# Where the two halves of an attention head's values are added: DVE out of the bank, or POOL in SBUF

## The chip, the cores and the metric

The kernel runs on one core of a Trainium2 chip. The metric is the device time of one execution in microseconds (us), the median of several runs. Five engines work side by side, each through its own instructions in order: TensorE (PE, with its weight loads shown as PEld), VectorE (DVE), ScalarE (ACT), GpSimd (POOL) and SyncE (SP, which issues DMAs here). They wait for each other through semaphores. Matrix products land in the banks of PSUM; all else lies in SBUF.

## The reference, cut to what matters

The program computes two layers of an encoder over 512 tokens of width 1024. In each layer, 12 token heads and 4 memory heads of width 64 attend, their outputs are concatenated, and one more product (`w_o`) follows. Layer 0 attends in a band of +-128 tokens with a sink logit, layer 1 globally with rotary and a norm on queries and keys.

```python
s = jnp.einsum('bqhgd,bkhd->bhgqk', qblk, k, preferred_element_type=jnp.float32) * ATTN_SCALE
p = jax.nn.softmax(s, axis=-1)
return jnp.einsum('bhgqk,bkhd->bqhgd', p.astype(v.dtype), v)
...
o = jnp.concatenate([tok, mo], axis=-1) @ w_o[i]
x = x + rms_norm(o, g_mix_post[i])
h = rms_norm(x, g_ffn_pre[i])
gu = h @ w_gate_up[i]
f = (jax.nn.silu(gu[..., :D_FF]) * gu[..., D_FF:]) @ w_down[i]
x = x + rms_norm(f, g_ffn_post[i])
```

## The kernel before, in words

Every operand of a product is split into a high part and a low part (`split`, L274: an ACT copy `hi` at L280 and a DVE subtraction `lo` at L284; for some weights both are on POOL, L278 and L282), and a product is three matmuls (L270 to L272). The order of the work in the attention stage is a list sorted by a position in heads, from the numbers in `PACE`; PE runs its instructions in the order in which that list is written, while the other engines' instructions are ordered by a scheduler.

One head passes through these steps, numbered 0 to 15 in each layer (12 to 15 are the memory heads, which have half as many keys and are paced closer together):

- `score` (L535) or `score_mem` (L566): PE writes the scores (L548, L549; L578, L579), DVE takes the minimum (L554, L559 or L580), ACT the exponential with the row sum (L560, L583).
- `normalise` (L589): DVE's reciprocal `rd` (L596), then four POOL multiplications of the probabilities `p` (L599). The four are the four blocks of 128 queries.
- `turn` (L602): PE transposes `p` (L609) into a bank `tp`, and `tp` is split into `th` on ACT (L280) and `tl` on DVE (L284). `turn` comes once for each block of 128 keys.
- `value` (L616): PE accumulates values times `th` and `tl` (L623, L624) in the bank `o`, of which there is one (tag `pv`, `bufs=1`). The values are stored as [high | low] in 64 + 64 columns, so that partitions 0 to 63 of `o` hold the high half of the output and 64 to 127 the low half. They must be added: ACT copies one half to the other's partitions in SBUF (`tmp`, L631, two buffers), and DVE adds it to the half that it reads from the bank, into `tok` (L632). Only then is the bank free for the next head's first L623.

Two heads share a slice `tok[:, k]` (k = 0 to 7). In `heads_out` (L765), once both are there, `part(k)` splits that slice into the operand of the `w_o` product, also called `th` in the profile: an ACT copy `th<-tok` (L280) and a DVE subtraction `th<-tok,th` (L284). The products of k = 0 to 5 with three of the four token blocks are mixed into the attention stage; `mix_out` (L796) does the fourth block of k = 0 to 5, then all four of k = 6, then of k = 7.

So ACT's queue holds, mixed: the exponentials, the splits of `tp`, the copies L631 and the splits of `tok`. DVE's holds the minima, the low parts and L632. POOL's holds L599 and, early in layer 0, splits of weights.

Of the kernel before, what the change touches and what calls it, by code (L numbers as in the profile page):

```python
# [13 lines left out]
OP = mybir.AluOpType  # L14
# [165 lines left out]
class Trunk:  # L180
# [435 lines left out]
    def value(self, hd, j):  # L616
        nc = self.nc
        if j == 0:
            hd["o"] = self.ps.tile([P, S], F32, tag="pv", name="o", bufs=1)
        o, hg = hd["o"], hd["hg"]  # L620
        c0, c1, th, tl = hd[j]
        last = j == hd["nk"] - 1
        nc.tensor.matmul(o[:, c0:c1], hd["v"](j), th, start=(j == 0), stop=False, skip_group_check=True)  # L623
        nc.tensor.matmul(o[:, c0:c1], hd["v"](j), tl, start=False, stop=last, skip_group_check=True)  # L624
        if not last:
            return
        odd = hg % 2
        here = slice(HD, P) if odd else slice(0, HD)
        there = slice(0, HD) if odd else slice(HD, P)
        tmp = self.core.tile([P, S], F32, tag="tmp", name="tmp", bufs=2)  # L630
        nc.scalar.activation(tmp[here], o[there], AF.Copy)  # L631
        nc.vector.tensor_add(self.tok[here, hg // 2], o[here], tmp[here])  # L632

    def axial(self, buf):

# [610 lines left out]
```

## Time and profile before

| | us |
|---|---|
| median of 3 runs (lowest to highest) | 1124.85 (1124.82 to 1125.47) |
| the profiled execution | 1125.38 |
| span of its instructions | 1123.6 |
| PE busy in the span | 1096.6 (98%) |
| DVE busy | 844.3 (75%) |
| ACT busy | 660.8 (59%) |
| POOL busy | 203.8 (18%) |

Times in rows of the trace are microseconds from the start of the span. In a row of the timeline stand the start, the time from the first start to the last end of a run of equal instructions, the engine, the line, what is written and read, the shape and the count; in square brackets the idle time of that engine ahead of it and what ended it. In a row of the groups stand the count, then the summed busy time and the mean duration of one in ns, then idle time. In the view of one tile, the lists below the rows give us in total and the number of times. The attention stages run from about 60 to 176 us (layer 0) and from about 600 to 745 us (layer 1).

### The profile page before, as it was taken

How to read it: one execution, taken by the hardware profiler on the slowest of the kernel's cores; microseconds unless marked ns; L12 is line 12 of the kernel's file. 1: busy time of each engine (PE TensorE's matmuls, PEld its weight loads, DVE VectorE, ACT ScalarE, POOL GpSimd, SP SyncE). 2: the span in 40 equal slices, each digit the busy share in tenths (PEclk: the TensorE clock that was granted, in tenths of full speed). 3: DMA queues.
4: the chain of work that ended last, by engine and by line, in shares of the span. 5: the costliest groups of instructions: out<-in, count | busy, mean ns of one | idle time of the engine just before them, and what ended most of it. 6: DMA issues, size and time to landing. Idle time of an engine off the chain costs nothing.

```text
span 1123.6 us, 19533 instructions
## 1 busy us (share of the span) xinstructions
PE 1096.6 (98%) x7463; PEld 1003.6 (89%) x7463; DVE 844.3 (75%) x1431; ACT 660.8 (59%) x1343; POOL 203.8 (18%) x348
## 2 busy tenths in 40 slices
PE   8999999999999999999999999999999999999997
PEld 7889988899889989998898888878999899899985
DVE  5688885899557867885788998758996478669854
ACT  6678984666445634663467878756665255345631
POOL 5693331102000000000343543312000000000001
PEclk9999999999999999999999999999999999999999
DMA  6521015443753382325543221145136223423243
GB/s 237 194 81 47 20 57 206 169 132 114 243 180 112 112 283 76 112 79 195 179 150 113 76 76 39 38 150 188 39 113 217 65 76 114 149 62 103 85 166 112
DMA packets 38685, 139.29 MB, mean 124 GB/s; under 512 B 4416, under 2 KB 4800, under 8 KB 38464
## 3 DMA queue, kind: packets, MB, share of 16 engines
q1 hardware_dynamic: 38448, 137.91, 36.4%
q8 instruction: 58, 0.95, 0.3%
q14 instruction: 35, 0.29, 0.1%
q10 hardware_dynamic: 144, 0.14, 0.0%
HBM read 119.16 MB, written 18.87 MB: 123 GB/s over the span
## 4 chain that ended last, share of the span: by engine, by line
PE 68%; DVE 6%; ACT 3%; POOL 2%; issue 2%; DVEq 0%; POOLq 0%; ACTq 0%
PE ps L978 12%; PE ps L979 12%; PE ps L980 12%; PE ps L271 9%; PE ps L270 9%; PE ps L272 9%; PE tp L609 1%; PE o L624 1%; PE o L623 1%; PE s L548 1%; DVE nm L559 1%; PE s L549 1%; DVE wlo L284 1%; POOL r L299 1%; ACT whi L280 1%
## 5 line engine op out<-in xcount | busy, mean ns | idle before, releaser
L280 ACT ACTIVATE whi<-raw 128x1024 fp32r<-128x1024 f32 (+2 forms) x186 | 157.9, 863 | 185.2 <-PE ps L980 81.8
L284 DVE TENSOR_TENSOR wlo<-raw,whi 128x1024 fp32r<-128x1024 f32 (+2 forms) x178 | 175.9, 998 | 74.8 <-ACT whi L280 71.7
L978 PE MATMUL ps<-sf,whi 128*128 128x256 f32 x640 | 179.9, 281 | 0.2
L979 PE MATMUL ps<-sf,wlo 128*128 128x256 f32 x640 | 179.7, 281 | 0.0
L980 PE MATMUL ps<-sf,whi 128*128 128x256 f32 x640 | 179.7, 281 | 0.0
L270 PE MATMUL ps<-whi,f 128*128 128x512 f32 x352 | 137.2, 390 | 0.0
L271 PE MATMUL ps<-wlo,f 128*128 128x512 f32 x352 | 137.1, 390 | 0.0
L272 PE MATMUL ps<-whi,f 128*128 128x512 f32 x352 | 137.0, 389 | 0.0
L980 PE MATMUL ps<-a,whi 128*128 128x256 f32 x480 | 134.4, 280 | 0.0
L978 PE MATMUL ps<-a,whi 128*128 128x256 f32 x480 | 134.3, 280 | 0.0
L979 PE MATMUL ps<-a,wlo 128*128 128x256 f32 x480 | 133.8, 279 | 0.0
L978 PEld LDWEIGHTS ps<-sf,whi 128*128 128x128 f32 x640 | 121.1, 189 | 1.1 <-ACT p L984 0.6
L979 PEld LDWEIGHTS ps<-sf,wlo 128*128 128x128 f32 x640 | 121.4, 190 | 0.5
L980 PEld LDWEIGHTS ps<-sf,whi 128*128 128x128 f32 x640 | 121.4, 190 | 0.0
L308 POOL TENSOR_SCALAR e<-sso 128x1 f32<-128x1 f32 x8 | 3.4, 424 | 566.1 <-ACT junk L303 565.9
L270 PE MATMUL ps<-whi,hT 128*128 128x256 f32 (+1 forms) x320 | 98.8, 309 | 0.9 <-ACT whi L292 0.9
L271 PE MATMUL ps<-wlo,hT 128*128 128x256 f32 (+1 forms) x320 | 93.9, 294 | 2.6 <-DVE wlo L284 1.9
L599 POOL TENSOR_SCALAR p<-p,rd 128x256 f32<-128x256 f32 (+2 forms) x128 | 78.2, 630 | 99.8 <-DVE rd L596 50.3
L272 PE MATMUL ps<-whi,hT 128*128 128x256 f32 (+1 forms) x320 | 93.7, 293 | 0.0
L979 PEld LDWEIGHTS ps<-a,wlo 128*128 128x128 f32 x480 | 90.5, 188 | 0.2
L978 PEld LDWEIGHTS ps<-a,whi 128*128 128x128 f32 x480 | 90.4, 188 | 0.2
L980 PEld LDWEIGHTS ps<-a,whi 128*128 128x128 f32 x480 | 90.1, 188 | 0.0
(201 smaller groups left out, 2735.0 us busy)
## 6 DMA issues: line engine op xcount, KB each, us to landing
raw<-in_wgu_dram SPq DMA_DIRECT2D x48, 512.0 KB, 4.4
raw<-in_wd_dram SPq DMA_DIRECT2D x44, 512.0 KB, 4.4
rb<-in_wgu_dram SPq DMA_DIRECT2D x40, 512.0 KB, 3.6
raw<-in_wo_dram SPq DMA_DIRECT2D x17, 512.0 KB, 3.6
raw<-in_wq_dram SPq DMA_DIRECT2D x16, 512.0 KB, 5.0
xt<-x SPq DMA_DIRECT2D x12, 512.0 KB, 4.5
raw<-in_wm_dram SPq DMA_DIRECT2D x8, 512.0 KB, 4.3
x<-y SPq DMA_DIRECT2D x8, 512.0 KB, 3.0
```

Of the source, the lines that this page charges most:

```text
L270: mm(out, lh, rh, start=first, stop=False)
L271: mm(out, lh, rl, start=False, stop=False)
L272: mm(out, ll, rh, start=False, stop=last)
L280: nc.scalar.activation(hi, src, AF.Copy)
L284: nc.vector.tensor_sub(lo, src, hi.bitcast(F32))
L299: g.tensor_tensor(r, r, self.mhalf[:, :r.shape[1]], op=OP.pow)
L548: nc.tensor.matmul(s[:, :n], qi, hd["ka"]()[:, k0 * P:k1 * P], start=True, stop=False)
L549: nc.tensor.matmul(s[:, :n], qi, hd["kb"]()[:, k0 * P:k1 * P], start=False, stop=True)
L599: self.pooled = nc.gpsimd.tensor_scalar(hd["p"][z][:, :n], hd["p"][z][:, :n], rd[:, z:z + 1], 1.0, op0=OP.mult, op1=OP.mult)
L978: mm(out, wh[:, s], rh, start=start and k == 0, stop=False, skip_group_check=True)
L979: mm(out, wl[:, s], rh, start=False, stop=False, skip_group_check=True)
L980: mm(out, wh[:, s], rl, start=False, stop=k == 3, skip_group_check=True)
```

## The change

The addition of the two halves leaves DVE. DVE copies its half from the bank to `tok` (L632), and POOL then adds `tmp` to it in SBUF, in place (a new line, L633; lines behind it move by one). The ACT copy L631 stays. That is 32 DVE additions replaced by 32 DVE copies of the same shape, and 32 POOL additions of 64x512 more.

```diff
         nc.scalar.activation(tmp[here], o[there], AF.Copy)
-        nc.vector.tensor_add(self.tok[here, hg // 2], o[here], tmp[here])
+        nc.vector.tensor_copy(self.tok[here, hg // 2], o[here])
+        nc.gpsimd.tensor_tensor(self.tok[here, hg // 2], self.tok[here, hg // 2], tmp[here], op=OP.add)
```

PE's instructions keep their order, and so do those of DVE and ACT but for one swap in each layer. POOL's change. Three places follow; in square brackets stand the engines whose counts an instruction waits for.

DVE in layer 0, from the L632 of head 11 on, before:

```order
L632 TENSOR_TENSOR tok<-o,tmp 64x512 [waits Activation_49]
L284 TENSOR_TENSOR tl<-tp,th 128x512 [waits DVE_49,Activation_49]
L580 TENSOR_REDUCE nm<-s 128x2 [waits PE_49]
L284 TENSOR_TENSOR th<-tok,th 128x512 [waits Activation_49]
L284 TENSOR_TENSOR tl<-tp,th 128x512 [waits Activation_49]
```

and after:

```order
L632 COPY tok<-o 64x512 [waits Activation_49]
L284 TENSOR_TENSOR tl<-tp,th 128x512 [waits DVE_49,Activation_49]
L580 TENSOR_REDUCE nm<-s 128x2 [waits PE_49]
L284 TENSOR_TENSOR th<-tok,th 128x512 [waits Activation_49]
L284 TENSOR_TENSOR tl<-tp,th 128x512 [waits DVE_49,Activation_49]
```

The copy stands where the addition stood. It reads nothing that ACT writes, and it still waits for ACT: the program makes it wait for the same count as before, the one that L631 of that head raises, and not for PE.

POOL in layer 0, at memory heads 14 and 15, before:

```order
L599 TENSOR_SCALAR p<-p,rd 128x256 [waits DVE_49]
L599 TENSOR_SCALAR p<-p,rd 128x256 [waits PE_49,Activation_49] x3
L599 TENSOR_SCALAR p<-p,rd 128x256 [waits DVE_49,PE_49]
L599 TENSOR_SCALAR p<-p,rd 128x256 [waits PE_49,Activation_49]
L599 TENSOR_SCALAR p<-p,rd 128x256 [waits Activation_49]
L599 TENSOR_SCALAR p<-p,rd 128x256 [waits PE_49,Activation_49]
```

and after, with the additions of heads 11, 12, 13 and of 14 and 15:

```order
L633 TENSOR_TENSOR tok<-tok,tmp 64x512 [waits DVE_49,Pool_49]
L599 TENSOR_SCALAR p<-p,rd 128x256 [waits DVE_49,PE_49,Pool_49]
L599 TENSOR_SCALAR p<-p,rd 128x256 [waits PE_49]
L599 TENSOR_SCALAR p<-p,rd 128x256 [waits PE_49,Activation_49] x2
L633 TENSOR_TENSOR tok<-tok,tmp 64x512 [waits DVE_49]
L599 TENSOR_SCALAR p<-p,rd 128x256 [waits DVE_49,PE_49]
L599 TENSOR_SCALAR p<-p,rd 128x256 [waits PE_49,Activation_49]
L599 TENSOR_SCALAR p<-p,rd 128x256 [waits Activation_49]
L599 TENSOR_SCALAR p<-p,rd 128x256 [waits PE_49,Activation_49]
L633 TENSOR_TENSOR tok<-tok,tmp 64x512 [waits DVE_49,Pool_49]
L633 TENSOR_TENSOR tok<-tok,tmp 64x512 [waits DVE_49] x2
```

The addition of head 13 stands behind the four multiplications of head 15, and each addition waits for DVE's copy.

ACT at the end of layer 0's attention, with the split of slice k = 7 (`th<-tok`) behind the last L631, before:

```order
L280 ACTIVATE th<-tp 128x512 [waits PE_49,Activation_49]
L631 ACTIVATE tmp<-o 64x512 [waits PE_49,Activation_49]
L280 ACTIVATE th<-tok 128x512 [waits DVE_49]
L280 ACTIVATE whi<-raw 128x512 [waits DMAHW7_49,PE_49]
L280 ACTIVATE whi<-raw 128x512
```

and after:

```order
L280 ACTIVATE th<-tp 128x512 [waits PE_49,Activation_49]
L631 ACTIVATE tmp<-o 64x512 [waits PE_49,Activation_49]
L280 ACTIVATE whi<-raw 128x512 [waits DMAHW7_49,PE_49]
L280 ACTIVATE th<-tok 128x512 [waits Pool_49]
L280 ACTIVATE whi<-raw 128x512
```

The split of `tok` now waits for POOL, and one piece of a weight's split has moved ahead of it; the same swap stands on DVE and in layer 1. The other splits of `tok` on ACT (k = 4, 5, 6) also wait for POOL where they waited for DVE, at the same places of ACT's queue as before.

## The prediction

> **What bounds the kernel now.** I read the page's head first:
>
> ```profile
> span 1123.6 us, 19533 instructions
> ...
> PE 1096.6 (98%) x7463; PEld 1003.6 (89%) x7463; DVE 844.3 (75%) x1431; ACT 660.8 (59%) x1343; POOL 203.8 (18%) x348
> ```
>
> PE is busy for 1096.6 of 1123.6 us, so 27 us of idle time is all that a change of order can win, and a microsecond that PE newly waits is a microsecond of the result. The change touches no PE instruction; it acts through what PE waits for. Then the view of the tile `tmp`, with the two instructions that empty the bank and those who wait for them:
>
> ```profile
> L631 ACT ACTIVATE tmp<-o x32: 589/594/597, 80.3 to 739.1; 64x512 f32<-64x512 f32 x32
> L632 DVE TENSOR_TENSOR tok<-o,tmp x32: 670/689/696, 81.0 to 739.7; 64x512 f32<-64x512 f32 x32
> ...
>   PEld o L623: 3.4, 6
>   PE o L623: 2.3, 5
> ```
>
> The bank is emptied in two steps of 0.59 and 0.69 us, one behind the other, and in all 32 heads PE's matmuls wait 2.3 us for that; the 3.4 us are waits of weight loads, which PE may or may not feel. So the bank's release is worth between 2.3 and 5.7 us at the very most.
>
> How full the engines are in the two attention stages shows the sum of a view by windows (80 to 176 and 615 to 745 us):
>
> ```profile
> sum 226.00, PE 219.20 PEld 192.19 DVE 190.41 ACT 185.89 POOL 87.11; mean PE 109.60 PEld 96.10 DVE 95.21 ACT 92.94 POOL 43.55
> ```
>
> PE idles 6.8 us of 226, DVE is busy for 84%, ACT for 82%, POOL for 39%. ACT and DVE work close behind PE, so a delay in their queues can reach it.
>
> **The DVE step.** The prices of the new operations come from the groups by shape:
>
> ```profile
> L282 POOL TENSOR_TENSOR wlo<-raw,whi 128x512 fp32r<-128x512 f32 x16 | 21.3, 1353 | 2.2 <-ACT whi L280 2.1
> ...
> L599 POOL TENSOR_SCALAR p<-p,rd 128x512 f32<-128x512 f32 x48 | 35.6, 759 | 29.6 <-DVE rd L596 24.3 <-PE s L579 5.4
> ```
>
> ```profile
> L415 DVE CAST kmb<-tp 128x512 fp32r<-128x512 f32 x4 | 2.7, 677 | 0.3 <-PE tp L414 0.3
> ```
>
> The nearest row to the new copy is that cast out of a bank: 512 columns in 0.68 us, hardly below the addition's 0.69. Twice the pace would show there as 0.34, and it does not. I take 0.68: 32 x 0.01 us, and only where PE waits; 0.1 us gained.
>
> What would matter is the start of the copy. "Side by side" means that it starts with L631 instead of behind it. The built program says no: the copy waits for the same count of ACT as the addition did. So the bank comes free when it did, the 2.3 us stay, and the change amounts to one more step behind an unchanged chain. [...]
>
> **The POOL step.** No row shows a POOL addition of 64x512. By columns its nearest row is L282, two inputs of 512 columns in SBUF: 1.35 us. From below it is bounded by L599, one input of 512 columns, 0.76 us. Half the partitions need not mean half the time: L631, at 64 partitions, takes 0.59 us, and ACT's copies of 128x512 below take 0.60 to 0.63. I take 1.35.
>
> That is 32 x 1.35 = 43 us more on POOL, in 226 us where it works 87. First, what is queued behind it on POOL: the next head's multiplications. In layer 0, head 2's copy and head 4's multiplications, with PE's first reads of these:
>
> ```profile
> 95.77 0.68 DVE L632 TENSOR_TENSOR tok<-o,tmp 64x512 f32<-64x512 f32 x1
> ...
> 97.31 2.11 POOL L599 TENSOR_SCALAR p<-p,rd 128x256 f32<-128x256 f32 x4 [4.47 <-ACT th L280]
> ...
> 100.77 0.39 PE L609 MATMUL tp<-cst,p 128*128 128x128 f32 x2
> ```
>
> The addition can start at 96.5 and ends at 97.85, so the multiplications start 0.5 us later. PE's reads at 100.77 need the first two of four, done by about 98.4: 2.3 us to spare. Token heads repeat this; cost 0, up to an addition of about 2.8 us.
>
> Second, who waits for POOL: the splits of `tok` on ACT. For k = 0 to 3 they come long after their heads. For k = 5 and 6 (in layer 1 for k = 4 too) they stand right behind the pair's second head, and ACT waits with all that is queued behind it. Place A, layer 0, k = 5:
>
> ```profile
> 158.40 0.69 DVE L632 TENSOR_TENSOR tok<-o,tmp 64x512 f32<-64x512 f32 x1 [1.17 <-ACT tmp L631]
> ...
> 159.13 0.63 ACT L280 ACTIVATE th<-tok 128x512 fp32r<-128x512 f32 x1
> ...
> 160.33 0.68 DVE L284 TENSOR_TENSOR th<-tok,th 128x512 fp32r<-128x512 f32 x1
> ...
> 160.41 0.60 ACT L280 ACTIVATE th<-tp 128x512 fp32r<-128x512 f32 x1 [0.65 <-PE tp L609]
> ...
> 162.51 1.85 POOL L599 TENSOR_SCALAR p<-p,rd 128x256 f32<-128x256 f32 x4 [5.13 <-DVE rd L596]
> ...
> 162.57 0.68 DVE L632 TENSOR_TENSOR tok<-o,tmp 64x512 f32<-64x512 f32 x1 [0.16 <-ACT tmp L631]
> ...
> 163.19 0.69 DVE L284 TENSOR_TENSOR tl<-tp,th 128x512 fp32r<-128x512 f32 x1
> ...
> 164.33 0.39 PE L624 MATMUL o<-tl,vm 128*128 128x512 f32 x1
> ...
> 164.56 0.60 PE L609 MATMUL tp<-cst,p 128*128 128x128 f32 x4
> ```
>
> The addition runs from 159.13 to 160.48, ACT's split starts at 160.51 instead of 159.13 and ends at 161.14. ACT's next is 0.6 us late. DVE's low half of the slice moves from 160.33 to 161.17, 0.84 late; DVE has no gap behind it, so the reciprocal and with it POOL's multiplications at 162.51 are 0.84 late and end at 165.20. The last of PE's four transposes at 164.56 starts at about 164.9 and needs the last of them: 0.3 late. L632 at 162.57 had waited 0.16 for ACT, so it and `tl` at 163.19 are 0.68 late, and L624 waits from 164.33 to 164.56. The two overlap; with the start behind a semaphore A costs 0.4 us.
>
> Place B, k = 6 of layer 0:
>
> ```profile
> 165.98 1.85 POOL L599 TENSOR_SCALAR p<-p,rd 128x256 f32<-128x256 f32 x4 [1.62 <-DVE rd L596]
> ...
> 167.57 0.63 ACT L280 ACTIVATE th<-tok 128x512 fp32r<-128x512 f32 x1
> ...
> 168.24 0.69 DVE L284 TENSOR_TENSOR th<-tok,th 128x512 fp32r<-128x512 f32 x1
> ...
> 169.15 0.60 ACT L280 ACTIVATE th<-tp 128x512 fp32r<-128x512 f32 x1 [0.95 <-PE tp L609]
> ...
> 169.79 0.69 DVE L284 TENSOR_TENSOR tl<-tp,th 128x512 fp32r<-128x512 f32 x1 [0.86 <-ACT th L280]
> ...
> 170.41 0.68 DVE L632 TENSOR_TENSOR tok<-o,tmp 64x512 f32<-64x512 f32 x1
> ...
> 171.15 0.50 PE L623 MATMUL o<-th,vm 128*128 128x512 f32 x1 [0.49 <-DVE tok L632]
> ```
>
> Here POOL is still at head 15's multiplications, which stand ahead of the addition: 167.83 + 1.35 = 169.2. DVE's low half moves from 168.24 to 169.87, `tl` from 169.79 to 170.57, L632 from 170.41 to 171.24: 0.83 late, and PE at 171.15 already waits for just that. What A left on the multiplications (0.65 late, of which PE's own 0.4 comes off) adds 0.25: B costs 1.05 us.
>
> Layer 1, k = 5 (place C), k = 6 (place D) and the end of the stage:
>
> ```profile
> 724.45 0.63 ACT L280 ACTIVATE th<-tok 128x512 fp32r<-128x512 f32 x1
> ...
> 725.84 0.47 ACT L583 ACTIVATE p<-s,nm 128x256 f32<-128x256 f32 x1 [0.75 <-DVE nm L580]
> ...
> 732.35 1.85 POOL L599 TENSOR_SCALAR p<-p,rd 128x256 f32<-128x256 f32 x4 [3.34 <-DVE rd L596]
> ...
> 733.66 0.64 ACT L280 ACTIVATE th<-tok 128x512 fp32r<-128x512 f32 x1
> ...
> 734.17 0.50 PE L624 MATMUL o<-tl,vm 128*128 128x512 f32 x1 [0.16 <-DVE tl L284]
> ...
> 736.55 0.68 DVE L632 TENSOR_TENSOR tok<-o,tmp 64x512 f32<-64x512 f32 x1 [1.25 <-ACT tmp L631]
> ...
> 737.38 0.47 PE L623 MATMUL o<-th,vm 128*128 128x512 f32 x1 [0.68 <-DVE tok L632]
> ```
>
> ```profile
> 741.14 0.69 DVE L284 TENSOR_TENSOR th<-tok,th 128x512 fp32r<-128x512 f32 x1 [0.70 <-ACT th L280]
> ...
> 745.86 0.40 PE L270 MATMUL ps<-whi,th 128*128 128x512 f32 x1
> ```
>
> C: the split goes from 724.45 to 725.85, the exponential behind it from 725.84 to 726.4, 0.55 late; between there and 734.17, where PE waits for DVE anyway, some of it is taken up by idle time. Between 0 and 0.55 I take 0.35. D: multiplications until 734.20, addition until 735.55, split until 736.2, DVE's low half (0.68 us) until 736.95, L632 0.37 late, and PE at 737.38 waits for it: 0.37. The last slice, k = 7, costs nothing: its low half would end some 1.4 us after 741.83, and the first matmul of k = 7 is the one at 745.86 (30 matmuls behind the last L624). Layer 1, k = 4 falls among token heads, whose 2.3 us to spare cover 1.4: 0.
>
> **DVE beside POOL.** Two low-half subtractions of 256 columns, the first with both inputs in SBUF, the second with one in a bank:
>
> ```profile
> L284 DVE TENSOR_TENSOR q<-qx,q 128x256 fp32r<-128x256 f32 x32 | 16.9, 528 | 4.0 <-ACT q L280 3.6
> ...
> L284 DVE TENSOR_TENSOR tl<-tp,th 128x256 fp32r<-128x256 f32 x24 | 10.0, 417 | 1.9 <-ACT th L280 1.7
> ```
>
> The first are 0.11 us slower, 3.5 us in 32. If that is POOL working beside them, 43 us more on 87 make half as much again: 1.8 us, and about as much for the rotary steps, 3.5 us of DVE time. DVE idles 16% of the stages, so most is covered: between 0 and 3.5 us I take 0.4. [...]
>
> **The sum.** 0.4 + 1.05 + 0.35 + 0.37 + 0.4 - 0.1 = 2.5 us. The profiled execution took 1125.38 us (its span and 1.8 us around it), which gives 1127.9; it lies 0.5 us above the median, so against 1124.85 the forecast is **1127.3 us**, with A to D uncertain by half: 1126.2 to 1128.6.
>
> **Rivals.**
>
> - *The two reads do overlap.* The bank would be free 0.6 us earlier and the splits would be 0.7 us late instead of 1.4: 2.3 us gained or a little more, about 1122.3. The program's wait speaks against it. 0.06.
> - *The addition is short* (not slower). ACT idles 0.65 us ahead of 160.41 and 0.95 ahead of 169.15. If POOL takes less than about 0.75 us for 64 partitions, the splits end before ACT's next instruction is due, and A to D vanish: 1124.9 to 1125.3. L599's 0.76 is near that point; that it has one input speaks against. 0.24.
> - *POOL becomes the bound.* If addition and DVE stretch each other, to 2 us each and 3.5 us of DVE, A to D grow by 0.65 each and 1 us of DVE time shows: 1127.3 + 2.6 + 0.6, about 1130.3. L282's mean was taken in just such company, which speaks against much more. 0.12.
>
> **How the numbers follow.** The forecast case has the remaining 0.58. About 0.2%, 2.25 us, is what a measurement of this kernel can tell from no change, so slower begins at 1127.1. Of the forecast's own range some two thirds lie above: slower 0.58 x 0.64 + 0.12 = 0.49, same 0.58 x 0.36 + 0.24 = 0.45, faster 0.06. The range from 1124.9 to 1130.0 takes in the short addition and most of the stretched one.
>
> **What would show it.** In the profile after: L632 as a copy of 0.67 to 0.69 us that starts behind L631 (if it starts with it, the first rival); L633 at 1.2 to 1.5 us on 64x512 (at 0.75 or less, the second); ACT's `th<-tok` waiting for POOL about seven times, over 1 us each; PE's idle time in the two stages up by about 2 us, at the memory heads and not at the token heads; q<-qx,q above 528 ns. PE waiting for L599 at token heads would make the place wrong, and a stage after the attention that takes up the delay would make the sum wrong.

## The result and the profile after

The changed kernel takes 1132.41 us (median of 4 runs, 1132.28 to 1132.91) against 1124.84 us before (4 runs beside it): ratio 1.0067, 95% interval 1.0049 to 1.0084, so 7.6 us slower. The forecast was 1127.3 us with a range up to 1130.0: the direction was right, the size was not. One execution of a later kernel (e6_dose1) had a mean granted clock of 0.56 and took 1795 us; it is left out of that kernel's time below, and all others ran at 0.996 or more.

The head of the page after:

```profile
span 1130.7 us, 19550 instructions
...
PE 1098.1 (97%) x7463; PEld 1003.5 (89%) x7463; DVE 852.1 (75%) x1431; ACT 660.7 (58%) x1343; POOL 244.3 (22%) x380
```

POOL has 40.5 us more work, as forecast (43). But DVE has 7.8 us more, although its copies were to be no longer than its additions. The view of the tile `tok`, after:

```profile
L632 DVE COPY tok<-o x32: 669/689/696, 80.6 to 747.0; 64x512 f32<-64x512 f32 x32
L633 POOL TENSOR_TENSOR tok<-tok,tmp x32: 1274/1287/1322, 82.2 to 747.8; 64x512 f32<-64x512 f32 x32
...
  POOL tok L633: 9.6, 7
...
  PE o L623: 3.4, 5
```

The copy takes 0.689 us, just what the addition took; POOL's addition takes 1.29; seven splits of `tok` on ACT wait for POOL, 1.4 us each; PE's wait for the bank grew from 2.3 to 3.4 us. None of that is 7.6 us. To find the place I compared the start of the same matmul in both traces (PE's order did not change):

| the matmul | before | after | later by |
|---|---|---|---|
| L270, near the start | 8.00 | 7.70 | -0.30 |
| L624, token heads, layer 0 | 85.52 | 86.97 | 1.45 |
| L609 | 98.08 | 101.39 | 3.31 |
| L609 | 111.81 | 116.33 | 4.52 |
| L609 | 119.01 | 124.63 | 5.62 |
| L609, memory heads (place A) | 164.88 | 170.92 | 6.04 |
| L623 (place B) | 171.15 | 178.08 | 6.93 |
| L623, token heads, layer 1 | 666.80 | 673.44 | 6.64 |
| L623, memory heads (place C) | 733.54 | 740.46 | 6.92 |
| L623 (place D) | 737.38 | 744.66 | 7.28 |

So 5.9 us are lost in token heads 0 to 7 of layer 0 (from 0.30 us early to 5.62 late), where the forecast had almost nothing, and 2.0 us at the four places that it named. What DVE does in that stretch shows the groups by shape, before (78 to 125 us):

```profile
L423 DVE TENSOR_TENSOR rt<-qx,cst 128x32 f32<-128x32 f32 x5 | 2.1, 415 | 0.0
L425 DVE TENSOR_TENSOR qx<-qx,rt 128x64 f32<-128x64 f32 x5 | 1.8, 362 | 0.1
L595 DVE TENSOR_TENSOR den<-den,es 128x4 f32<-128x4 f32 x7 | 1.4, 199 | 0.2
L424 DVE TENSOR_TENSOR qx<-qx,cst 128x64 f32<-128x64 f32 x5 | 1.3, 270 | 0.0
...
L422 DVE TENSOR_TENSOR rt<-qx,cst 128x32 f32<-128x32 f32 x5 | 1.0, 195 | 0.0
```

and after (78 to 131 us):

```profile
L422 DVE TENSOR_TENSOR rt<-qx,cst 128x32 f32<-128x32 f32 x5 | 5.3, 1058 | 0.0
...
L424 DVE TENSOR_TENSOR qx<-qx,cst 128x64 f32<-128x64 f32 x5 | 2.4, 475 | 0.0
L425 DVE TENSOR_TENSOR qx<-qx,rt 128x64 f32<-128x64 f32 x5 | 2.3, 451 | 0.1
L595 DVE TENSOR_TENSOR den<-den,es 128x4 f32<-128x4 f32 x7 | 2.2, 320 | 0.2
...
L423 DVE TENSOR_TENSOR rt<-qx,cst 128x32 f32<-128x32 f32 x5 | 1.3, 267 | 0.0
```

L422 to L425 are the rotary step of the next four heads' queries (layer 0 has one too, on 16 of a head's 64 columns); in this stretch of layer 0 it comes five times, once in each of heads 0 to 4. They, L595 and the low part `q<-qx,q` read two operands in SBUF. L422 went from 0.20 to 1.06 us. With that low part (0.42 to 0.50 us, seven of them) the six groups, each count times the change of its mean, have 6.5 us more. The timeline of one head, after, shows why. PE, waiting, stands in the last row:

```profile
99.25 0.16 DVE L595 TENSOR_TENSOR den<-den,es 128x4 f32<-128x4 f32 x1
99.33 1.29 POOL L633 TENSOR_TENSOR tok<-tok,tmp 64x512 f32<-64x512 f32 x1 [3.68 <-DVE tok L632]
99.37 0.48 DVE L554 CUSTOM_DVE_ANT_0 p<-s,mask,nsink 128x256 f32<-128x256 f32 x1
...
99.87 0.80 DVE L422 TENSOR_TENSOR rt<-qx,cst 128x32 f32<-128x32 f32 x1
...
101.39 0.41 PE L609 MATMUL tp<-cst,p 128*128 128x128 f32 x2 [0.35 <-DVE qx L424]
```

The addition runs from 99.33 to 100.62. L422, which needs 0.16 us, starts at 99.87 and ends at 100.67, right behind it. L554 between them reads `s` in a bank and `mask` in SBUF; it takes 0.48 us inside the addition, as it does without it. In all five heads L422 ends 0.05 to 0.07 us behind the end of a POOL instruction with two inputs. In head 5, which has no L422, L595 took 1.01 us and ended 0.02 behind the addition. The worst is the first L422, where another such POOL instruction follows at once:

```profile
82.25 1.28 POOL L633 TENSOR_TENSOR tok<-tok,tmp 64x512 f32<-64x512 f32 x1
...
82.58 2.27 DVE L422 TENSOR_TENSOR rt<-qx,cst 128x32 f32<-128x32 f32 x1
83.49 1.29 POOL L282 TENSOR_TENSOR wlo<-raw,whi 128x512 fp32r<-128x512 f32 x1
...
86.97 0.44 PE L624 MATMUL o<-tl,vs 128*128 128x384 f32 x1 [1.93 <-DVE tl L284]
```

My theory (P): the addition starts behind the same L632 as DVE's next work, so the rotary step meets it in every head that has one and is held to its end; DVE's queue there has little slack, so the hold reaches PE. Its rivals: the time is POOL's and the waits for it (O), or the waits of ACT's splits of `tok` (W).

### The profile page after: what moved, and what is told of

Read it like the earlier page. It is cut to its first block, busy times and chain, and to the rows that moved or that the text cites. A ratio compares the mean times of both kernels' runs of the same rounds, so it can differ in the third digit from the quotient of the medians.

```text
span 1130.7 us, 19550 instructions
## 1 busy us (share of the span) xinstructions
PE 1098.1 (97%) x7463; PEld 1003.5 (89%) x7463; DVE 852.1 (75%) x1431; ACT 660.7 (58%) x1343; POOL 244.3 (22%) x380
## 4 chain that ended last, share of the span: by engine, by line
PE 78%; DVE 9%; ACT 5%; POOL 4%; issue 2%; DMA 1%; SPq 0%; POOLq 0%; DVEq 0%; ACTq 0%
PE ps L979 12%; PE ps L271 12%; PE ps L981 12%; PE ps L980 12%; PE ps L270 12%; PE ps L272 12%; PE tp L609 2%; PE o L624 1%; PE o L623 1%; DVE tl L284 1%; PE s L548 1%; PE s L549 1%; POOL p L599 1%; ACT whi L280 1%; ACT junk L303 1%
## 5 line engine op out<-in xcount | busy, mean ns | idle before, releaser
L980 PE MATMUL ps<-sf,wlo 128*128 128x256 f32 x640 | 179.7, 281 | 0.0
L270 PE MATMUL ps<-whi,f 128*128 128x512 f32 x352 | 137.2, 390 | 0.0
L980 PE MATMUL ps<-a,wlo 128*128 128x256 f32 x480 | 133.8, 279 | 0.0
L980 PEld LDWEIGHTS ps<-sf,wlo 128*128 128x128 f32 x640 | 121.3, 190 | 0.5
L270 PE MATMUL ps<-whi,hT 128*128 128x256 f32 (+1 forms) x320 | 98.7, 308 | 0.5 <-ACT whi L292 0.5
L980 PEld LDWEIGHTS ps<-a,wlo 128*128 128x128 f32 x480 | 90.5, 188 | 0.2
L599 POOL TENSOR_SCALAR p<-p,rd 128x256 f32<-128x256 f32 (+2 forms) x128 | 78.1, 628 | 45.7 <-DVE rd L596 25.6
```

The source lines that it names most:

```text
L270: mm(out, lh, rh, start=first, stop=False)
L599: self.pooled = nc.gpsimd.tensor_scalar(hd["p"][z][:, :n], hd["p"][z][:, :n], rd[:, z:z + 1], 1.0, op0=OP.mult, op1=OP.mult)
L980: mm(out, wl[:, s], rh, start=False, stop=False, skip_group_check=True)
```

## The experiments

Each kernel is the kernel before with the edit shown (`self.layer` is a name for the layer's number). Intervals are at 95%.

| run | us | before beside it | ratio (interval) |
|---|---|---|---|
| e1_early | 1131.00 | 1124.32 | 1.0059 (1.0044 to 1.0074) |
| e2_rest | 1125.87 | 1124.32 | 1.0014 (1.0004 to 1.0023) |
| e3_four | 1126.48 | 1124.32 | 1.0019 (1.0009 to 1.0028) |
| e4_one | 1127.28 | 1124.32 | 1.0028 (1.0017 to 1.0040) |
| e5_dose0 | 1126.62 | 1124.52 | 1.0019 (1.0010 to 1.0028) |
| e6_dose1 | 1127.15 | 1124.52 | 1.0023 (1.0013 to 1.0032) |
| e7_phase | 1128.52 | 1124.52 | 1.0034 (1.0022 to 1.0046) |
| e8_whole | 1127.18 | 1124.52 | 1.0024 (1.0015 to 1.0033) |
| e9_phase2 | 1125.95 | 1124.41 | 1.0014 (1.0005 to 1.0023) |
| e10_whole1 | 1121.77 | 1124.41 | 0.9977 (0.9968 to 0.9986) |
| e11_whole1b | 1122.62 | 1124.41 | 0.9985 (0.9976 to 0.9994) |
| e12_whole2 | 1123.75 | 1124.71 | 0.9993 (0.9984 to 1.0002) |

**Which heads cost.** Three kernels make the change for a part of the heads. The condition is `self.layer == 0 and hg < 8` in the first, `self.layer == 1 or hg >= 8` in the second, `hg in (11, 13)` in the third:

```diff
-        nc.vector.tensor_add(self.tok[here, hg // 2], o[here], tmp[here])
+        if self.layer == 0 and hg < 8:
+            nc.vector.tensor_copy(self.tok[here, hg // 2], o[here])
+            nc.gpsimd.tensor_tensor(self.tok[here, hg // 2], self.tok[here, hg // 2], tmp[here], op=OP.add)
+        else:
+            nc.vector.tensor_add(self.tok[here, hg // 2], o[here], tmp[here])
```

> DVE copy and POOL addition only for heads 0 to 7 of layer 0 (8 additions); the other 24 heads keep DVE's addition. Theory P (DVE's rotary step L422, two inputs in SBUF, is held until POOL's addition that began behind the same copy has ended, once in each head): +5.0 to +6.0 us over the kernel before, L422 in the token heads at 0.7 to 0.8 us instead of 0.16, and 2.3 once where two POOL instructions follow each other. Theory W (the loss comes from ACT's splits of tok waiting for POOL): within 0.5 us of before, since the slices k = 0 to 3 are split long after their heads. Theory O (POOL has too much to do in all, so the loss is spread over all additions): a quarter of 7.5, about +1.9 us.

> The opposite choice: DVE's addition for heads 0 to 7 of layer 0, copy and POOL addition in the other 24 heads. Theory P: only the waits of the tok splits A to D are left, +1.3 to +2.3 us, and PE loses nothing in token heads 0 to 7. Theory W: the whole loss, +7 us. Theory O: three quarters of it, about +5.6 us.

> Copy and POOL addition only for heads 11 and 13 of both layers (4 additions), those right ahead of the splits of k = 5 and k = 6. Theory P with the forecast's places A to D: +1.5 to +2.2 us (0.41 + 0.90 + 0.29 + 0.35 as the kernel after shows them), each at its place. Theory O: an eighth, about +0.9 us. If A to D are themselves a contention of DVE and POOL and not a wait of ACT: under +0.7 us.

Eight of the 32 additions cost 6.7 us (0.7 above the range of theory P), the other 24 together 1.55 us. That rules out O and W as the main cause. In the first, L422 has the mean of the kernel after:

```profile
L422 DVE TENSOR_TENSOR rt<-qx,cst 128x32 f32<-128x32 f32 x5 | 5.3, 1057 | 0.0
```

The four additions ahead of the late splits cost 2.15 us, and the trace places it: PE is 1.0 us later at place B, 0.45 more at C and 0.3 more at D. The 20 further additions of the second add nothing that can be told from zero.

**The meeting, or POOL's time?** The fourth kernel is the kernel after with two POOL multiplications by 1 in place of the addition (it leaves out the half in `tmp`); its edit is shown against the kernel after:

```diff
         nc.vector.tensor_copy(self.tok[here, hg // 2], o[here])
-        nc.gpsimd.tensor_tensor(self.tok[here, hg // 2], self.tok[here, hg // 2], tmp[here], op=OP.add)
+        for _ in range(2):
+            nc.gpsimd.tensor_scalar(self.tok[here, hg // 2], self.tok[here, hg // 2], 1.0, 1.0, op0=OP.mult, op1=OP.mult)
```

> The copy as in the kernel after, but POOL's addition in all 32 heads is replaced by two POOL multiplications by 1 with one input each, in place on tok (leaves out the addition of the half in tmp), which take about as long together, 1.2 to 1.5 us. Theory P (two inputs on POOL hold DVE's instruction with two inputs): L422 goes back to 0.16 to 0.2 us, the loss in layer 0's token heads goes, and A to D stay, +1.3 to +2.5 us in all. Theory O (POOL's time and the waits for it): +7 to +8 us, as after. If one input on POOL is enough to hold DVE: L422 at 0.5 to 0.8 and +5 us or more.

POOL is as busy as in the kernel after (245.0 us), and the seven waits of ACT are there (9.2 us). But the loss is 2.96 us, a little above what P gave. Of L422's five, three took 0.16 us, one 0.19, and the first 1.60, held by the old L282. Its sum, in 78 to 131 us:

```profile
L422 DVE TENSOR_TENSOR rt<-qx,cst 128x32 f32<-128x32 f32 x5 | 2.3, 454 | 0.0
```

So it is neither POOL's busy time nor the waits for it. But this run does not show that it takes two inputs on POOL to hold DVE, as I had put theory P for it. L422 started just as the first multiplication ended; L423 behind it, which needs 0.18 us, met the second:

```profile
89.70 1.32 POOL L634 TENSOR_SCALAR tok<-tok 64x512 f32<-64x512 f32 x2 [1.19 <-DVE tok L632]
...
90.36 0.16 DVE L422 TENSOR_TENSOR rt<-qx,cst 128x32 f32<-128x32 f32 x1
90.43 0.63 DVE L423 TENSOR_TENSOR rt<-qx,cst 128x32 f32<-128x32 f32 x1
```

The multiplications end at 91.02, L423 at 91.06. The kernel before shows the same in most places: of 43 DVE instructions with two inputs in SBUF that began 0.05 us or more behind the start of a POOL instruction with one input (of 192 columns or more), and at least 0.15 us ahead of its end, 39 ended right behind that end, by 0.04 us with 32 columns, 0.07 with 64, 0.27 with 256 and 0.54 with 512. So one input on POOL holds DVE too; what this run took away is the length of the hold.

The sharper test keeps the additions as they are and moves them. In the seventh kernel, in heads 0 to 7 of layer 0, POOL first copies one column of the next query piece's low part, and the addition is issued behind that:

```diff
                 self.split(st["q2"][:, :, :HD], st["q2"][:, :, HD:P], qx)
+                if self.due:
+                    e = self.small.tile([P, 1], F32, tag="e8", name="e8", bufs=2)
+                    mark = nc.gpsimd.tensor_scalar(e, st["q2"][:, 3, P - 1:P].bitcast(F32), 1.0, 1.0, op0=OP.mult, op1=OP.mult)
+                    with self.tc.issue_after(mark.ins):
+                        nc.gpsimd.tensor_tensor(self.due[0], self.due[0], self.due[1], op=OP.add)
+                    self.due = None
...
-        nc.vector.tensor_add(self.tok[here, hg // 2], o[here], tmp[here])
+        if self.layer == 0 and hg < 8:
+            nc.vector.tensor_copy(self.tok[here, hg // 2], o[here])
...
+            self.due = self.tok[here, hg // 2], tmp[here]
+        else:
+            nc.vector.tensor_add(self.tok[here, hg // 2], o[here], tmp[here])
```

> As the run with copy and POOL addition in heads 0 to 7 of layer 0 only, but each addition first waits for the low part of the next piece of queries (a POOL copy of one column of q2 ahead of it), so that it falls in the 3 us in which DVE's instructions read a bank. As many additions of the same length, on the same engine. Theory P (what costs is the meeting with the rotary step): L422 back to 0.16 to 0.2 us and +0.0 to +1.0 us over the kernel before. Theory O (POOL's time): +5 to +6 us as in that run.

It took 4.0 us more than before, but most of it not where the additions are: at 137 us PE is 1.2 us late, and between two matmuls of layer 1's feed-forward stage (830 and 1060 us) it lost 2.2 us (232.2 us instead of 230.0). There the matmuls L978 to L980, which wait for nothing, each took 1 to 2 ns longer. The ninth kernel writes the column to an unused place of `q2` instead of the new tile:

```diff
-                    e = self.small.tile([P, 1], F32, tag="e8", name="e8", bufs=2)
-                    mark = nc.gpsimd.tensor_scalar(e, st["q2"][:, 3, P - 1:P].bitcast(F32), 1.0, 1.0, op0=OP.mult, op1=OP.mult)
+                    mark = nc.gpsimd.tensor_scalar(st["q2"][:, 3, P:P + 1], st["q2"][:, 3, P - 1:P].bitcast(F32), 1.0, 1.0, op0=OP.mult, op1=OP.mult)
```

> As the run with the additions put behind the low part of the queries in heads 0 to 7 of layer 0, but the one column that POOL copies goes to an unused column of q2 and not to a small tile of its own, since in that run the matmuls L978 to L980 of layer 1's feed-forward stage, far behind the change, each took 1 to 2 ns longer (2.2 us in all). If that came from the new tile's place in SBUF, it is gone here: +0.3 to +1.5 us in all, L422 at 0.16 to 0.2 us (theory P). If it came with the later addition itself: +3.5 to +4.5 us. Theory O (POOL's time): +5.5 us or more.

The feed-forward stage is back at 230.0 us, and the loss is 1.5 us where the same eight additions in their first place cost 6.7. One head of its timeline, to be held against the one of the kernel after:

```profile
96.35 0.16 DVE L422 TENSOR_TENSOR rt<-qx,cst 128x32 f32<-128x32 f32 x1
...
98.71 0.42 DVE L284 TENSOR_TENSOR q<-qx,q 128x256 fp32r<-128x256 f32 x1
...
99.38 0.60 DVE L559 CUSTOM_DVE_ANT_0 p<-s,mask,nsink 128x384 f32<-128x384 f32 x1
99.43 1.28 POOL L520 TENSOR_TENSOR tok<-tok,tmp 64x512 f32<-64x512 f32 x1
```

The addition is as long as before and lies beside instructions of DVE that read a bank; L422 is back at 0.16 us. The same work on the same engines costs 5 us less in another place: theory P holds.

**How much of a hold reaches PE.** Two kernels put one more DVE instruction, with one input in SBUF, into heads 0 to 7 of layer 0 or of layer 1, and nothing on POOL:

```diff
         nc.vector.tensor_add(self.tok[here, hg // 2], o[here], tmp[here])
+        if self.layer == 0 and hg < 8:
+            nc.vector.tensor_scalar(self.tok[here, hg // 2], self.tok[here, hg // 2], 1.0, 1.0, op0=OP.mult, op1=OP.mult)
```

> The kernel before, with one more DVE instruction behind L632 in heads 0 to 7 of layer 0: tok times 1 in place, 64x512, one input in SBUF; nothing on POOL. It takes d us (to be read; 0.35 to 0.7). Theory P says that DVE's queue there has no slack, so that a hold of DVE passes to PE nearly in full (about 6 us of held DVE time made 5.9 us in the kernel after): +0.8 to +1.0 times 8 d, so +2.2 to +5.6 us. Theory C (DVE idles 16% of the stage and covers it, as the forecast had it): under 0.2 times 8 d, so less than +1 us.

> The same DVE instruction in heads 0 to 7 of layer 1, where the kernel after lost nothing. Theory M (nothing was lost there only because POOL's additions met no DVE instruction with two inputs in SBUF; DVE is as tight as in layer 0): +0.6 to +1.0 times 8 d. Theory S (DVE has slack in layer 1, so that a hold there would be hidden too): under 0.2 times 8 d.

The instruction took 0.41 us in layer 0 (8 of them are 3.3 us) and 0.46 in layer 1 (3.7 us); they cost 2.1 and 2.6 us. So some two thirds of DVE's time pass to PE in both layers: in layer 0 below what P said (0.8 to 1.0, which the interval of 1.1 to 3.1 us still reaches), and in both above the fifth that a covered engine would show, even at the low ends of the intervals (1.1 and 1.5 us). And layer 1 lost nothing in its token heads because the additions met little there, not because DVE had time.

**A version without the cost.** If DVE's time is worth two thirds in token heads, the way to gain is to take L632 off DVE altogether. Here ACT copies the whole bank in one instruction, POOL brings the other half across, and POOL adds, behind the same column of the next queries as in the seventh kernel:

```diff
+        if hg < 8:
+            nc.scalar.activation(tmp, o, AF.Copy)
+            nc.gpsimd.tensor_scalar(self.tok[here, hg // 2], tmp[there], 1.0, 1.0, op0=OP.mult, op1=OP.mult)
...
+            self.due = self.tok[here, hg // 2], tmp[here]
+        else:
...
```

> A version that aims at the change's end without its costs, in heads 0 to 7 of both layers: ACT copies the whole bank (128x512) to tmp in one instruction, DVE does nothing, POOL brings the other half across (one input) and adds behind the low part of the queries as in the run before. DVE is rid of 0.69 us in each of 16 heads and the bank is free 0.69 us earlier. Theory P: no hold by the addition, a smaller one by the one-input copy (up to 0.3 us each); PE idles only some 2 us in these stretches, so -1.5 to +1.0 us. If one input on POOL holds DVE as two do: +2 us or more.

It took 2.7 us more than before. 2.2 us of that are the feed-forward stage again (it has the small tile of the seventh kernel); of the rest, layer 0 lost and layer 1 gained: at 667 us PE was 1.1 us ahead of the kernel before. So the next one does it in layer 1 alone (`self.layer == 1 and hg < 8`), with the column in `q2`:

> ACT's copy of the whole bank, POOL's copy across and POOL's addition behind the low part of the queries, in heads 0 to 7 of layer 1 only (the mark as in the run above); layer 0 as before. In the run with both layers PE gained 2.8 us on the kernel before between 601 and 667 us. Theory P (no hold, DVE rid of 8 x 0.69 us where its time passes to PE): -3.0 to -1.5 us. If that gain was only given back from layer 0's delay: within 0.7 us of before.

It is the fastest: 1121.77 us, 2.6 us below the kernel before. Two windows of 20 us in layer 1's token heads, of the kernel before:

```profile
650.00:670.00 20.00, 19.13 (x131) 16.69 (x130) 19.08 (x38) 15.82 (x38) 8.91 (x12) 1.00 0.31 106
```

and of this one, 4 us earlier because it is that far ahead (PE, PEld, DVE, ACT, POOL, with the number of instructions):

```profile
646.00:666.00 20.00, 20.00 (x140) 17.91 (x139) 17.92 (x37) 16.61 (x40) 15.53 (x23) 1.00 0.33 106
```

DVE's 19.1 of 20 us have become 17.9, POOL's 8.9 have become 15.5, and PE is never idle. ACT's single copy (0.60 us, where L631 and L632 took 0.59 and 0.69 one behind the other) also frees the bank earlier, which could be the gain instead; but what PE waited for in the kernel before, from 625 to 690 us (us in total, times, longest), was hardly the bank:

```profile
PE tp L609 <- DVE tl L284: 1.2, 2, 0.6
PE o L623 <- DVE tok L632: 0.2, 1, 0.2
```

In the tenth kernel that list is empty. Two further variants do more of it. The first puts both POOL instructions at once behind ACT's copy, in heads 0 to 10 of layer 1; the second adds layer 0's heads 0 to 7, both POOL instructions behind the column:

> The same for heads 0 to 10 of layer 1, with both POOL instructions one behind the other as soon as the copy is there, ahead of the next L298 and L299. If the meeting with DVE decides: DVE's L444 and q<-qx,q are held by the addition or wait for L299 up to 1.9 us later, and half or more of the gain is lost, -1.2 to +1.5 us. If it does not matter where the addition falls in layer 1: -3.5 to -1.5 us.

> The faster version of layer 1 (heads 0 to 7) kept, and the same in layer 0's heads 0 to 7 with both POOL instructions, the copy across and the addition (1.9 us together), behind the low part of the queries, in the 3 us in which DVE reads banks. In the earlier run with both layers the copy across stood beside the rotary step, and layer 0 lost about 2 us. Theory P: L422 at 0.16 to 0.2 us; DVE rid of 8 x 0.69 us there, of which a little over half passes to PE, but PE idles only 1.6 us there: layer 0 gains 0.3 to 1.5 us, so -4.3 to -2.9 us against the kernel before. If POOL's time itself costs in layer 0: slower than the version with layer 1 alone, -2.0 us or less.

Neither did better, and my expectation of the last one was wrong. The eleventh gains as much as the tenth up to the matmul that stood at 690 us (4.04 and 4.07 us ahead, both a microsecond ahead from the start), so in heads 0 to 6 of layer 1 the place did not matter; behind that (heads 7 to 10) it loses about 1 us to it. The twelfth is not to be told from the kernel before: layer 1 gains 2.3 us in its trace (2.50 us late at 601 us, 0.24 at 734), but layer 0 loses 1.5 us up to 139 us (from 0.18 early to 1.37 late). Its rows there:

```profile
134.42 0.62 POOL L521 TENSOR_SCALAR tok<-tmp 64x512 f32<-64x512 f32 x1
134.46 1.11 DVE L284 TENSOR_TENSOR th<-tok,th 128x512 fp32r<-128x512 f32 x1
135.12 1.61 POOL L522 TENSOR_TENSOR tok<-tok,tmp 64x512 f32<-64x512 f32 x1
...
136.04 1.25 DVE L284 TENSOR_TENSOR th<-tok,th 128x512 fp32r<-128x512 f32 x1
...
138.77 0.52 PE L616 MATMUL tp<-cst,p 128*128 128x128 f32 x3 [1.16 <-DVE den L602]
```

The POOL instructions of head 7 now meet the low parts of `tok`, which also read two operands in SBUF and take 0.69 us in the kernel before: the first ends 0.53 us behind the copy across (one input), the second 0.56 behind the addition (0.54 behind for 512 columns in the kernel before), the same hold with another victim. In the eleventh kernel one of these took 1.82 us, from 689.62 on, beside an addition that began at 689.61, and its loss to the tenth begins 4 us behind that. My expectation had a rival here, that POOL's time itself costs in layer 0, and by its number the twelfth came out on that side; the rows speak for the hold, but no run tests it.

A further 1.3 us of this trace, just behind, is neither; that it belongs to the clock is my estimate from the two rows below. From 140 to 144 us PE is busy throughout, and the granted clock, the number behind the five engines, is 0.69 and then 0.50:

```profile
140.00:142.00 2.00, 2.00 (x9) 1.72 (x10) 1.92 (x6) 2.00 (x8) 1.75 (x3) 0.69 0.00 0
142.00:144.00 2.00, 2.00 (x7) 1.71 (x6) 0.41 (x2) 1.57 (x4) 0.00 (x0) 0.50 0.03 8
```

That execution took 1126.16 us, 2.4 above the median of its kernel. Without that stretch the trace's gain and loss, 2.3 and 1.5 us, leave some 0.8 us won, near the 1.0 that the medians give.

## Why the prediction was wrong, point by point

- *The DVE step* (0.1 us gained): the copy waits for L631 and does not start earlier, as said. It takes 0.689 us and not 0.68, so nothing is gained. The first rival, overlapping reads, did not occur: in all 32 heads of the kernel after the copy starts 0.03 us or more behind the end of L631. That the program could be made to let the two reads overlap was not tried.
- *The POOL step*: 1.29 us against 1.35 taken. The second rival needed less than 0.75. The multiplications L599 did start later, and PE's wait for them stayed at 1.8 us in 3 times: the 2.3 us to spare covered it.
- *Places A to D* (0.4, 1.05, 0.35, 0.37): the table gives 0.42, 0.89, 0.28 and 0.36, together 1.95 against 2.17. The chain was the one described. Place B, after, with POOL behind the multiplications, ACT behind POOL and PE behind DVE:

```profile
174.16 1.29 POOL L633 TENSOR_TENSOR tok<-tok,tmp 64x512 f32<-64x512 f32 x1
175.47 0.63 ACT L280 ACTIVATE th<-tok 128x512 fp32r<-128x512 f32 x1 [1.91 <-POOL tok L633]
...
178.08 0.50 PE L623 MATMUL o<-th,vm 128*128 128x512 f32 x1 [1.35 <-DVE tok L632]
```

- *DVE beside POOL* (0.4 us): this is the step that failed. It measured 5.9 us. It said "between 0 and 3.5 us I take 0.4", because "DVE idles 16% of the stages, so most is covered". Three things were wrong in it. The price came from means: 0.11 us for each low part `q<-qx,q`. A hold is no such share; it lasts until POOL's instruction has ended, and rows of the kernel before showed that, as this one of L423, whose minimum is 0.18 us:

```profile
83.17 1.34 DVE L423 TENSOR_TENSOR rt<-qx,cst 128x32 f32<-128x32 f32 x1
83.17 1.29 POOL L282 TENSOR_TENSOR wlo<-raw,whi 128x512 fp32r<-128x512 f32 x1
```

  Next, I counted meetings as if they fell by chance. The addition and the rotary step both start from L632, so they meet in every head where both are there, which is heads 0 to 4 of layer 0 (5 of 32; in head 5 it was L595), and elsewhere hardly at all. And the cover was an average over both stages: where the meetings fall, two thirds and more of DVE's time passes to PE.
- *"At the memory heads and not at the token heads"*: wrong for the same reason; three quarters of the loss lie at the token heads.
- *POOL becomes the bound* (1130.3): the nearest of the rivals, still 2.1 us short (its own terms, 1127.3 + 2.6 + 0.6, make 1130.5), and not by its mechanism: additions were not stretched (1.29 us), and A to D did not grow.

What stays open: when DVE is let in between two POOL instructions that follow each other at once (the last section has both outcomes). And the sum of the parts, 6.7 + 1.55 us, is 0.7 above the 7.6 of the whole; the intervals (about 1.7 us wide either way for the first) cover that.

## What to carry to other kernels

Before work is moved from DVE to POOL, list DVE's instructions with two inputs in SBUF that follow the same event, and price each as held until POOL's instruction ends, as most were here for one input on POOL (39 of 43) and for two (all five L422 of the kernel after); one long row in the trace of before (L423, 1.34 us against 0.18 at its shortest) says more than the mean of its group. With the fixed order here such a meeting came in all five heads with a rotary step, so where the moved work stands in the queue can be worth more than how long it takes: the same eight additions cost 6.7 us in one place and 1.5 in another. And a copy out of a bank was no cheaper here than an addition out of it (0.689 us each), so a change of this kind relieves DVE only if it takes the whole instruction away, in a stage where DVE is the engine that PE waits for.

## What the runs showed of the hardware

- DVE instructions with two inputs in SBUF that started while a POOL instruction was under way mostly ended just behind it, for one input on POOL (39 of 43 in the kernel before) as for two (L422 in all five heads of the kernel after). In three of the four others it was POOL's instruction that took long (1.07, 1.42 and 0.66 us, against 0.58, 0.47 and 0.35 at the shortest), and L443 took its usual 0.42 us beside POOL's L299 of 4 columns in five places. DVE instructions that read a bank were as long beside POOL as without it: `tl<-tp,th` of 384 columns took 0.55 us at the median in both cases in the kernel before, and the copy L632 0.68 and 0.69 in the kernel after.
- POOL's addition of 64x512 takes 1.29 us, and its subtraction of 128x512 1.30 at the median: half the partitions, the same time.
- A DVE instruction that needs 0.16 us took 2.27 us beside two POOL instructions with two inputs that stand back to back: it ended 0.07 us behind the second. Elsewhere it got in between: at 55.28 us of the kernel before, L422 took 0.51 us and ended at 55.79, 0.05 behind the first of two L282 that stand back to back.
- A new tile of one column (two buffers), in use only in the attention stage, made some 1,300 matmuls of a stage 700 us later (L978 to L980) slower by 1 to 2 ns each, 2.2 us in all, and without the tile they were as before. Why is not shown.
- In the trace of e12_whole2 the granted clock was 0.69 from 140 to 142 us and 0.50 from 142 to 144, soon after a wait of PE of 1.16 us (at 138.77). The trace of the kernel after has a longer wait, 1.93 us ahead of 86.97, and there the clock stayed at 1.00 from 84 to 94 us. Why it falls is not shown.
